# A place of its own for each weight slab: shifted split weights in a decoder step of one core

## The chip, the core and the metric

The kernel runs on one core of a Trainium2 chip. The core has a matrix engine (TensorE), three engines that work on vectors (VectorE, ScalarE, GpSimd), SyncE, which here issues the transfers, and 16 DMA engines. Data are worked on in an on-chip memory of 128 partitions; TensorE writes its sums to a second one, PSUM. The metric is the time of one execution in microseconds on the device, as the median of several runs: 1639.8 us before the change (three runs, 1639.6 to 1639.88).

## What is computed

One step of a decoder layer for 288 token rows (a prompt of 256 and 8 samples of 4), all float32:

```
h = RMSNorm(x);  P = h @ w_in          # split into conv, stick-breaking attention, memory attention, gates
y_A, y_B, y_M                           # three branches, each ending in a projection to D_MODEL = 2048
x = x + (g_A*y_A + g_B*y_B + g_M*y_M) @ w_o
x = x + relu(RMSNorm(x) @ w_up)^2 @ w_down      # D_FF = 8192
```

Beside it, the keys and values of 256 memory tokens are projected, and new cache rows are returned. Nearly all the work is the product of 288 columns of activations with weights that are read once.

## The kernel before, in words

**Slabs.** All weights lie in one array `wall` of 504 slabs, each 128 partitions by 1024 float32 (512 KB). A slab holds eight blocks of 128x128. Slabs 0 to 15 belong to the memory keys and values, 16 to 215 to w_in and the branch projections, 216 to 247 to w_o. From 248 on four rounds follow, each with an up stage (32 slabs of w_up) and a down stage (32 slabs of w_down): up stages at 248, 312, 376 and 440, down stages at 280, 344, 408 and 472.

**The split.** Products of full float32 precision are made of the reduced type fp32r. A weight w is written as h + l: `cast_weights` (line 303, ScalarE) casts the raw slab `wr` into a tile `wh`, and `sub_part` (line 314, VectorE) writes the rest, wr - wh, into `wl`. Activations are split in the same way into `.h` and `.l`. A block's product is three matmuls: wh with a.h, wh with a.l, wl with a.h. So a slab is 8 x 3 = 24 matmuls. They stand on line 486, in `chunk`, first the 16 with wh, then the 8 with wl; each loads 128 columns of weights and streams the 288 columns of an activation. The memory stage (line 539) does it the other way round: 128 columns of an activation are the weights, and 512 columns of wh or wl stream.

**The buffers.** There are four raw slabs (`wr`), four `wh` and four `wl`, used in turn. Activations lie in pool `a` (tiles of 320 words), where class `Acts` takes words 12 to 300 (`AHEAD = 12`) for the 288-column ones. After the branches the tiles of the pools `k4` and `s` are made into 16 "homes", pairs of places for an h and an l half (`make_homes`): the merged branches use them as the input of w_o, and each up stage writes its output into them (`up_tile`), which the down stage reads. The pools' sizes, a spare tile `gap` of 32 words among them, and the 12 words put the moving operand of every line-486 matmul 48 bytes in front of its weights, counted modulo 256 bytes; for the memory stage the distance is 0.

**The order.** The whole program is written in the order that a planner (`Order`) works out when the kernel is built: each step is a generator that asks for an engine with a cost, flags to wait for and buffers. The matmuls of `main` stand in their fixed order; the other engines' steps are placed by these costs. Weights are loaded by SyncE in slab order as raw buffers come free, and a `wh`/`wl` buffer is given back when its slab's last matmul is written.

Names in the profile: `pm` and `pa` are PSUM banks, `a` activations, `k` and `s` the homes, `t` temporaries.

Of the kernel before, what the change touches and what calls it, by code (L numbers as in the profile page):

```python
# [7 lines left out]
F32 = mybir.dt.float32  # L8
F32R = mybir.dt.float32r
# [5 lines left out]
P = 128  # L15
D_MODEL = 2048
KT = D_MODEL // P
# [4 lines left out]
T = NP + NS  # L22
# [13 lines left out]
SLAB = 8 * P  # L36
N_SLABS = 504
# [116 lines left out]
def dve(n, *flags, **take):  # L154
    return Ask("DVE", 0.18 + n / 920.0, flags, **take)


def act(n, *flags, **take):
    return Ask("ACT", 0.22 + n / 1200.0, flags, **take)
# [12 lines left out]


APART = 320
AHEAD = 12
VISIT, VISIT_K = 4, 8
MM = 0.131
MM_MEM = 0.226
# [3 lines left out]
def tile_decoder_step(ctx: ExitStack, tc: tile.TileContext, xT, memT, wall, cvec, kmat, ptab,  # L182
                      kpool, vpool, mkc, mvc, hist,
                      yT, oK, oV, oCp, oCs, oMK, oMV):
    nc = tc.nc
    PS = bass.MemoryType.PSUM
    bufs = {"wr": 4, "w": 4, "a": 75, "t": 11, "k4": 9, "s": 8, "pm": 4, "pa": 3, "pl": 1}

    def open_pool(name, n, space=None):
        if space is None:  # L190
            return ctx.enter_context(tc.tile_pool(name=name, bufs=n))
        return ctx.enter_context(tc.tile_pool(name=name, bufs=n, space=space))

    cpool = open_pool("const", 1)
    pools = {}
    for p, n in bufs.items():
        if p == "t":
            open_pool("gap", 1).tile([P, 32], F32, name="gap")
        if p != "w":
            pools[p] = open_pool(p, n, PS if p in ("pm", "pa", "pl") else None)  # L200
    pools["wh"] = open_pool("wh", bufs["w"])
# [6 lines left out]
    def tl(p, shape, dt=F32):  # L208
        cnt[0] += 1
        return pools[p].tile(shape, dt, tag=p, name=f"{p}_{cnt[0]}")  # L210
# [16 lines left out]


    nc.scalar.preload_act_table_set(LN_EXP)
    warm = pools["wh"].tile([P, SLAB], F32R, tag="wh", name="wh_0")  # L230
    order.pools["w"].pop()
    nc.gpsimd.memset(warm[:, :512].bitcast(F32), 1.0)
    eps = cpool.tile([P, 1], F32, name="eps")
    nc.gpsimd.memset(eps, EPS)
    ones = cpool.tile([P, P], F32, name="ones")
    nc.gpsimd.memset(ones, 1.0)
    ones_r = cpool.tile([P, P], F32R, name="ones_r")
    nc.vector.tensor_copy(ones_r, ones)
    ones_s = cpool.tile([P, T], F32, name="ones_s")
    nc.gpsimd.memset(ones_s, 1.0)  # L240
    cv = cpool.tile([P, NCV], F32, name="cv")
    nc.scalar.dma_start(cv[:, :C_BGATE], cvec[:, :C_BGATE])
    km = cpool.tile([P, NKM], F32, name="km")
# [4 lines left out]
    snew = km[:, K_SNEW:K_SNEW + NS]  # L248
    tri_r = cpool.tile([P, P], F32R, name="tri_r")
    rx = cpool.tile([P, T], F32, name="rx")  # L250
    r2 = cpool.tile([P, T], F32, name="r2")
    rm = cpool.tile([P, MT], F32, name="rm")
    nm = [cpool.tile([P, MT * MH], F32, name=f"nm{i}") for i in range(4)]
    sm_mx, sm_sum, sm_rc = (cpool.tile([P, 2], F32, name=f"sm{i}") for i in range(3))
# [25 lines left out]
    def load_slab(s, part):  # L280
# [4 lines left out]
        nc.sync.dma_start(sl.raw[:, part * n:(part + 1) * n], wall[s, :, part * n:(part + 1) * n])  # L285
        sl.landed[part].at = order.landed(n * P * 4 / 1e3)

    def due(s):
        return at_slab[1] + 2.9 * (s - at_slab[0])

# [2 lines left out]
    def cast_weights():  # L293
        todo = [(0, 0), (1, 0), (0, 1), (1, 1)] + [(s, i) for s in range(2, N_SLABS) for i in range(slabs[s].parts)]
        for s, i in todo:
            sl = slabs[s]
            n = SLAB // sl.parts
            cast_at[0] = s
            yield act(n, sl.landed[i], **({} if i else {"w": 1}))
            if i == 0:  # L300
                sl.h = tl("wh", [P, SLAB], F32R)
            c = slice(i * n, (i + 1) * n)
            nc.scalar.copy(sl.h[:, c], sl.raw[:, c])  # L303
            sl.split[i].cast = order.now.ready
            add(sub_part(s, i), lambda s=s: 0 if due(s) - order.free["DVE"] < 5.0 else 4.5)

    def sub_part(s, i):
        sl = slabs[s]
        n = SLAB // sl.parts
        yield dve(n, late=Order.HOP + 0.1)  # L310
        if i == 0:
            sl.l = tl("wl", [P, SLAB], F32R)
        c = slice(i * n, (i + 1) * n)
        nc.vector.tensor_sub(sl.l[:, c], sl.raw[:, c], sl.h[:, c].bitcast(F32))  # L314
        done(sl.split[i])
        if i == sl.parts - 1:
            give("wr")
# [5 lines left out]
    class Acts:  # L323


        def __init__(self, n=T):
            c = slice(AHEAD, AHEAD + n) if n == T else slice(0, n)
            self.h, self.l = tl("a", [P, APART], F32R)[:, c], tl("a", [P, APART], F32R)[:, c]
            self.flag = Flag()

# [176 lines left out]
    def main_tile(acts, evac, rank=1.0, n_slabs=2):  # L507
        yield pe(0.0, pm=1)
        ps = bank("pm")[:, :T]
        for i in range(n_slabs):  # L510
            slab_no[0] += 1
            yield from products(ps, FULL, acts[8 * i:8 * i + 8], i == 0, i == n_slabs - 1)
            give("w")
        add(evac(ps), rank)
# [720 lines left out]
    homes, homes_in = [], Flag()  # L1235
# [4 lines left out]

    def make_homes():
        yield sp(*conv_done, *osb_in, k4=bufs["k4"], s=bufs["s"])
        parts = []
        for _ in range(bufs["k4"]):
            x = tl("k4", [P, 1024], F32R)
            parts += [x[:, AHEAD + i * APART:AHEAD + i * APART + T] for i in range(3)]
        for _ in range(bufs["s"]):
            parts.append(tl("s", [P, 512], F32R)[:, AHEAD:AHEAD + T])
        for j in range(KT):
            homes.append(Home(parts[2 * j], parts[2 * j + 1]))  # L1250
        done(homes_in)


# [12 lines left out]
    merged = [None] * KT  # L1266

    def branch(br, j):
        def evac(ps):
            sig = gates[br, j]  # L1270
            if br == 2:
                yield dve(T, sig.flag, a=1)
                macc[j] = tl("a", [P, T])
                nc.vector.tensor_mul(macc[j], ps, sig.out)
                give("pm")
                give("t")
                return
            yield dve(T, sig.flag)
            nc.vector.tensor_mul(sig.out, ps, sig.out)
            give("pm")  # L1280
            yield dve(T)
            nc.vector.tensor_add(macc[j], macc[j], sig.out)
            give("t")
            if br == 0:
                yield act(T, homes_in)
                a = merged[j] = homes[j]
                nc.scalar.copy(a.h, macc[j])
                yield dve(T)
                nc.vector.tensor_sub(a.l, macc[j], a.h.bitcast(F32))
                give("a")  # L1290
                done(merged_in[j])
        return evac
# [41 lines left out]
        return load, evac  # L1334


    def up_tile(u, f):
        def evac(ps):
            yield dve(T, r2_done, t=1)
            r = tl("t", [P, T])  # L1340
            nc.vector.scalar_tensor_tensor(r, ps, 0.0, r2, op0=ALU.max, op1=ALU.mult)  # L1341
            give("pm")
            yield pool(T)
            nc.gpsimd.tensor_mul(r, r, r)  # L1344
            yield act(T)
            a = homes[f]
            nc.scalar.copy(a.h, r)  # L1347
            yield dve(T)
            nc.vector.tensor_sub(a.l, r, a.h.bitcast(F32))  # L1349
            give("t")  # L1350
            u[f].h, u[f].l = a.h, a.l
            done(u[f].flag)
        return evac
# [57 lines left out]
    def main():  # L1411
        yield from warm_up()
        yield from mem_products()
        yield from conv_products([evac_lin(0, "pa"), evac_gat(0, "pa"), evac_lin(1, "pm"), evac_gat(1, "pm")])
        for j in range(2, CT):
            yield from main_tile(hx, evac_lin(j, "pm"))
            yield from main_tile(hx, evac_gat(j, "pm"))
        add(samples(), 3.0)
        for h in range(MH):
            yield from main_tile(hx, mem_head(h), 2 + 0.05 * h)  # L1420
        for h in range(SH):
            yield from main_tile(hx, sb_key(h), 2.2 + 0.05 * h)
            yield from main_tile(hx, sb_query(h), 2.2 + 0.05 * h)
            yield from main_tile(hx, sb_head(h), 2.2 + 0.05 * h)
        yield from branch_products(2, [Late(omem, h, om_in[h]) for h in range(MH)])
        give("a", 8)
        yield from branch_products(1, [Late(osb, h, osb_in[h]) for h in range(SH)])
        give("a", 16)
        yield from branch_products(0, [Late(cact, j, cact_flags[j]) for j in range(CT)])
        give("a", 40)  # L1430
        mg = [Late(merged, j, merged_in[j]) for j in range(KT)]
        for j in range(KT):
            load, evac = out_tile(j)
            add(load(), 2)
            yield from main_tile(mg, evac)
        add(sum_norm(sq_sum, D_MODEL, r2, r2_done, sums_2), 0.4)
        hh = [Late(h2, j, h2_in[j]) for j in range(KT)]
        for c in range(D_FF // D_MODEL):
            u = [Later() for _ in range(KT)]
            for f in range(KT):  # L1440
                yield from main_tile(hh, up_tile(u, f))
            for j in range(KT):
                yield from main_tile(u, down_tile(j, c == D_FF // D_MODEL - 1))

# [174 lines left out]
```

## Time and profile before

| | |
|---|---|
| median of three runs | 1639.8 us |
| the profiled execution | 1639.4 us, its span 1637.6 us |
| TensorE matmuls | 12786, busy 1633.0 us (100%) |
| weight loads of TensorE | 12786, busy 1615.7 us (99%) |
| VectorE | 992.2 us (61%) |
| ScalarE | 739.3 us (45%) |
| GpSimd | 138.9 us (8%) |
| DMA | 305.39 MB, mean 186 GB/s |
| granted TensorE clock | 1.000 |

The span is the time from the first to the last instruction of the profiled execution; its own time has a little more around it. A matmul's record lasts from the start of its reading to the end of its writing, and the next one starts well before that; so the pace of matmuls is read from their starts, not from the durations. In rows of the chain and of the order in time, the first number is the start of a piece in us from the span's start, the second its length, and the number behind the x how many instructions it merges.

### The profile page before, as it was taken

How to read it: one execution, taken by the hardware profiler on the slowest of the kernel's cores; microseconds unless marked ns; L12 is line 12 of the kernel's file. 1: busy time of each engine (PE TensorE's matmuls, PEld its weight loads, DVE VectorE, ACT ScalarE, POOL GpSimd, SP SyncE). 2: the span in 40 equal slices, each digit the busy share in tenths (PEclk: the TensorE clock that was granted, in tenths of full speed). 3: DMA queues.
4: the chain of work that ended last, by engine and by line, in shares of the span. 5: the costliest groups of instructions: out<-in, count | busy, mean ns of one | idle time of the engine just before them, and what ended most of it. 6: DMA issues, size and time to landing. Idle time of an engine off the chain costs nothing.

```text
span 1637.6 us, 30963 instructions
## 1 busy us (share of the span) xinstructions
PE 1633.0 (100%) x12786; PEld 1615.7 (99%) x12786; DVE 992.2 (61%) x1471; ACT 739.3 (45%) x1070; POOL 138.9 (8%) x105
## 2 busy tenths in 40 slices
PE   9999999999999999999999999999999999999999
PEld 7999999999999999999999999999999999999999
DVE  8888888877777655565555544455445554455443
ACT  8746666644343534444443433333333333333332
POOL 0020000000000000001222200122001210022100
PEclk9999999999999999999999999999999999999999
DMA  9686465776755555556655555555555555555563
GB/s 339 217 184 248 148 203 195 251 257 243 256 162 167 152 184 174 169 162 202 193 175 167 170 169 173 170 168 170 167 169 168 169 173 170 169 168 168 179 192 100
DMA packets 107103, 305.39 MB, mean 186 GB/s; under 512 B 19922, under 2 KB 29522, under 8 KB 106962
## 3 DMA queue, kind: packets, MB, share of 16 engines
q1 hardware_dynamic: 106818, 303.39, 58.4%
q8 instruction: 100, 1.64, 0.4%
q14 instruction: 41, 0.34, 0.1%
q10 hardware_dynamic: 144, 0.02, 0.0%
HBM read 297.05 MB, written 6.32 MB: 185 GB/s over the span
## 4 chain that ended last, share of the span: by engine, by line
PE 100%; POOL 0%; DVE 0%; issue 0%; POOLq 0%
PE pm L486 93%; PE pm L539 3%; PE pa L486 1%; PE pl L1015 1%; PE pl L1188 0%; PE pa L852 0%; PE pa L853 0%; PE pa L851 0%; PE pl L1031 0%; PE pa L1407 0%; PE pa L825 0%; PE pa L1142 0%; PE pa L906 0%; PE pa L1139 0%; PE pa L1141 0%; PE pa L1106 0%
## 5 line engine op out<-in xcount | busy, mean ns | idle before, releaser
L303 ACT CAST wh<-wr 128x1024 fp32r<-128x1024 f32 (+1 forms) x520 | 530.5, 1023 | 652.1 <-PE pm L486 596.2
L486 PE MATMUL pm<-a,wh 128*128 128x288 f32 x5184 | 742.3, 293 | 0.0
L314 DVE TENSOR_TENSOR wl<-wr,wh 128x1024 fp32r<-128x1024 f32 (+1 forms) x520 | 616.6, 1189 | 197.2 <-ACT wh L303 192.4
L486 PEld LDWEIGHTS pm<-a,wh 128*128 128x128 f32 x5184 | 699.7, 188 | 1.3 <-issue 1.2
L486 PE MATMUL pm<-a,wl 128*128 128x288 f32 x2592 | 398.6, 293 | 0.0
L486 PEld LDWEIGHTS pm<-a,wl 128*128 128x128 f32 x2592 | 359.8, 188 | 0.0
L486 PE MATMUL pm<-k,wh 128*128 128x288 f32 x2160 | 306.8, 292 | 0.0
L486 PEld LDWEIGHTS pm<-k,wh 128*128 128x128 f32 x2160 | 290.2, 188 | 0.0
L486 PE MATMUL pm<-k,wl 128*128 128x288 f32 x1120 | 171.6, 292 | 0.0
L486 PEld LDWEIGHTS pm<-k,wl 128*128 128x128 f32 x1120 | 155.0, 188 | 0.0
L1344 POOL TENSOR_TENSOR t<-t 128x288 f32<-128x288 f32 x64 | 96.3, 1505 | 599.9 <-DVE t L1341 599.9
L1358 DVE TENSOR_TENSOR a<-a,pm 128x288 f32<-128x288 f32 x64 | 29.1, 454 | 122.5 <-PE pm L486 122.5
L1341 DVE SCALAR_TENSOR_TENSOR t<-pm,r 128x288 f32<-128x288 f32 x64 | 29.2, 458 | 90.3 <-PE pm L486 90.3
L1347 ACT CAST k<-t 128x288 fp32r<-128x288 f32 x56 | 24.2, 433 | 115.7 <-POOL t L1344 115.7
L1260 DVE TENSOR_TENSOR t<-pm,rx 128x288 f32<-128x288 f32 x48 | 22.0, 458 | 73.2 <-PE pm L486 73.2
L486 PE MATMUL pm<-s,wh 128*128 128x288 f32 x400 | 65.0, 293 | 0.0
L717 DVE SCALAR_TENSOR_TENSOR a<-a,cv,a 128x256 f32<-128x256 f32 x120 | 57.7, 481 | 1.4
L1330 POOL TENSOR_TENSOR t<-t,t 128x288 f32<-128x288 f32 x15 | 22.0, 1469 | 420.9 <-ACT t L1327 420.9
L486 PEld LDWEIGHTS pm<-s,wh 128*128 128x128 f32 x400 | 56.6, 188 | 0.0
L1349 DVE TENSOR_TENSOR k<-t,k 128x288 fp32r<-128x288 f32 x52 | 23.8, 458 | 51.1 <-ACT k L1347 51.1
L539 PE MATMUL pm<-wh,a 128*128 128x512 f32 x128 | 35.1, 396 | 0.0
L486 PE MATMUL pm<-s,wl 128*128 128x288 f32 x160 | 33.8, 293 | 0.0
(214 smaller groups left out, 785.5 us busy)
## 6 DMA issues: line engine op xcount, KB each, us to landing
wr<-in_wall SPq DMA_DIRECT2D x488, 512.0 KB, 3.6
wr<-in_wall SPq DMA_DIRECT2D x32, 256.0 KB, 4.8
k<-in_kpool SPq DMA_DIRECT2D x32, 256.0 KB, 6.0
k<-in_vpool SPq DMA_DIRECT2D x32, 256.0 KB, 5.9
k<-in_mkc SPq DMA_DIRECT2D x8, 512.0 KB, 8.8
k<-in_mvc SPq DMA_DIRECT2D x8, 512.0 KB, 6.4
t<-in_xT SPq DMA_DIRECT2D x16, 144.0 KB, 3.6
out_yT<-a SPq DMA_DIRECT2D x16, 144.0 KB, 1.8
```

The source lines that it names most:

```text
L303: nc.scalar.copy(sl.h[:, c], sl.raw[:, c])
L314: nc.vector.tensor_sub(sl.l[:, c], sl.raw[:, c], sl.h[:, c].bitcast(F32))
L486: nc.tensor.matmul(ps, w, a, start=(first and i == 0), stop=(last and i == len(todo) - 1))
L539: nc.tensor.matmul(ps[m], y[:, m * P:(m + 1) * P], z[:, w], start=(k == 0 and j < 2), stop=(k == KT - 1 and j in (4, 5)))
L717: nc.vector.scalar_tensor_tensor(c[:, :NP], up[:, k:k + NP], w, c[:, :NP], op0=ALU.mult, op1=ALU.add)
L1260: nc.vector.tensor_mul(g, ps, rx)
L1330: nc.gpsimd.tensor_add(sq_sum[0], sq_sum[0], res[0])
L1341: nc.vector.scalar_tensor_tensor(r, ps, 0.0, r2, op0=ALU.max, op1=ALU.mult)
L1344: nc.gpsimd.tensor_mul(r, r, r)
L1347: nc.scalar.copy(a.h, r)
L1349: nc.vector.tensor_sub(a.l, r, a.h.bitcast(F32))
L1358: nc.vector.tensor_add(x1[j], x1[j], ps)
```

## The change

Three things change together, all of them places of data in the partition.

- `wh` and `wl` buffers are 64 words (256 bytes) longer, and a table `SHIFT` gives the number of words by which each of the last 288 slabs (216 on) is moved forward in its buffers, the same for wh and wl.
- The activations' places: `AHEAD` is 4, the tile `gap` is gone, and the 16 homes exist in five sets of places (`PLACES`), one for w_o and one for each of the four rounds, with a start of its own for the h and the l half.
- To make room, the tile `ones` is dropped (its copy is read from `ones_s`), and `r2` uses the tile of `rx`.

As a result, counted modulo 256 bytes from the weights to the moving data: in slabs 16 to 215 the distance is 144 bytes instead of 48. In the first up stage it takes turns by slab between 144 and 96, in the second between 144 and 48, in the third between 96 and 48. In w_o, the four down stages and the last up stage it is given by lot. In w_o and the down stages each of 16 shifts, 16 bytes apart, occurs twice; in the last up stage the eight shifts 0, 5, 7, 11, 30, 32, 39 and 55 words occur four times each. The memory stage stays at distance 0.

No instruction changes its place in the order of TensorE, ScalarE, VectorE or SyncE; GpSimd has one fill fewer.

```diff
-AHEAD = 12
+AHEAD = 4
+PLACES = ((6, 6), (4, 12), (12, 4), (4, 0), (2, 2))
+SHIFT = (
+    10, 62, 34, 30, 54, 22, 30, 18, 38, 38, 18, 58, 26, 50, 62, 42, 58, 42, 34, 6, 2, 22, 54, 14,
+    26, 14, 46, 6, 46, 50, 2, 10, 0, 12, 0, 12, 0, 12, 0, 12, 0, 12, 0, 12, 0, 12, 0, 12,
...
+)
+PAD = 64
...
-        if p == "t":
-            open_pool("gap", 1).tile([P, 32], F32, name="gap")
...
-    warm = pools["wh"].tile([P, SLAB], F32R, tag="wh", name="wh_0")
+    warm = pools["wh"].tile([P, SLAB + PAD], F32R, tag="wh", name="wh_0")
...
-    ones = cpool.tile([P, P], F32, name="ones")
-    nc.gpsimd.memset(ones, 1.0)
-    ones_r = cpool.tile([P, P], F32R, name="ones_r")
-    nc.vector.tensor_copy(ones_r, ones)
     ones_s = cpool.tile([P, T], F32, name="ones_s")
     nc.gpsimd.memset(ones_s, 1.0)
+    ones_r = cpool.tile([P, P], F32R, name="ones_r")
+    nc.vector.tensor_copy(ones_r, ones_s[:, :P])
...
-    r2 = cpool.tile([P, T], F32, name="r2")
+    r2 = rx
...
+    def shifted(p, s):
+        n = SHIFT[s - N_SLABS + len(SHIFT)] if s >= N_SLABS - len(SHIFT) else 0
+        return tl(p, [P, SLAB + PAD], F32R)[:, n:n + SLAB]
...
-                sl.h = tl("wh", [P, SLAB], F32R)
+                sl.h = shifted("wh", s)
...
-            sl.l = tl("wl", [P, SLAB], F32R)
+            sl.l = shifted("wl", s)
...
-            c = slice(AHEAD, AHEAD + n) if n == T else slice(0, n)
+            c = slice(AHEAD, AHEAD + n) if n == T else slice(32, 32 + n)
...
-        for _ in range(bufs["k4"]):
-            x = tl("k4", [P, 1024], F32R)
-            parts += [x[:, AHEAD + i * APART:AHEAD + i * APART + T] for i in range(3)]
-        for _ in range(bufs["s"]):
-            parts.append(tl("s", [P, 512], F32R)[:, AHEAD:AHEAD + T])
-        for j in range(KT):
-            homes.append(Home(parts[2 * j], parts[2 * j + 1]))
+        big = [tl("k4", [P, 1024], F32R) for _ in range(bufs["k4"])]
+        small = [tl("s", [P, 512], F32R) for _ in range(bufs["s"])]
+        for place in PLACES:
+            parts = [[x[:, i * APART + n:i * APART + n + T] for x in big for i in range(3)] + [x[:, n:n + T] for x in small]
+                     for n in place]
+            homes.append([Home(parts[0][2 * j], parts[1][2 * j + 1]) for j in range(KT)])
...
-                a = merged[j] = homes[j]
+                a = merged[j] = homes[0][j]
...
-            a = homes[f]
+            a = homes[1 + c][f]
```

More of the change, by code (lines that the diff above doesn't have):

```diff
@@ L1242, in make_homes @@
         yield sp(*conv_done, *osb_in, k4=bufs["k4"], s=bufs["s"])
-        parts = []
-        for _ in range(bufs["k4"]):
-            x = tl("k4", [P, 1024], F32R)
-            parts += [x[:, AHEAD + i * APART:AHEAD + i * APART + T] for i in range(3)]
-        for _ in range(bufs["s"]):
-            parts.append(tl("s", [P, 512], F32R)[:, AHEAD:AHEAD + T])
-        for j in range(KT):
-            homes.append(Home(parts[2 * j], parts[2 * j + 1]))
+        big = [tl("k4", [P, 1024], F32R) for _ in range(bufs["k4"])]
[4 more added lines that the diff above has]
+            homes.append([Home(parts[0][2 * j], parts[1][2 * j + 1]) for j in range(KT)])
         done(homes_in)
@@ L1334, in out_tile, with up_tile @@
         return load, evac
-    def up_tile(u, f):
+    def up_tile(u, f, c):
         def evac(ps):
@@ L1440, in main @@
             for f in range(KT):
-                yield from main_tile(hh, up_tile(u, f))
+                yield from main_tile(hh, up_tile(u, f, c))
             for j in range(KT):
```

10 rows, old and new, of the table SHIFT are left out of this document.

## The prediction

> **What bounds the kernel now.** I read the page first (busy shares), then the chain that ended last in order of time, then the order of single instructions on TensorE, and last the groups of ScalarE and VectorE.
>
> ```profile
> span 1637.6 us, 30963 instructions
> ...
> PE 1633.0 (100%) x12786; PEld 1615.7 (99%) x12786; DVE 992.2 (61%) x1471; ACT 739.3 (45%) x1070; POOL 138.9 (8%) x105
> ...
> PEclk9999999999999999999999999999999999999999
> ...
> PE 100%; POOL 0%; DVE 0%; issue 0%; POOLq 0%
> PE pm L486 93%; PE pm L539 3%; PE pa L486 1%; PE pl L1015 1%; PE pl L1188 0%; PE pa L852 0%; PE pa L853 0%; PE pa L851 0%; PE pl L1031 0%; PE pa L1407 0%; PE pa L825 0%; PE pa L1142 0%; PE pa L906 0%; PE pa L1139 0%; PE pa L1141 0%; PE pa L1106 0%
> ```
>
> TensorE is busy for the whole span at full clock, and the chain is TensorE alone: 94% of it the matmuls of line 486, each 128 weight columns against 288 moving columns. The only thing that can move the time by much is the pace of those matmuls, that is the time from one start to the next. The next rows (start, length, instructions of a piece of the chain) give it.
>
> ```profile
> 364.66 29.41 PE pm L486 x222
> ...
> 439.71 84.27 PE pm L486 x636
> 524.24 22.26 PE pm L486 x168
> 546.77 297.18 PE pm L486 x2286
> 844.22 790.16 PE pm L486 x6078
> ```
>
> 84.27/636 = 132.5 ns, 29.41/222 = 132.5 and 22.26/168 = 132.5; but 297.18/2286 = 130.0 and 790.16/6078 = 130.0. The same instruction, with operands at the same distance in the partition, runs at one of two paces, and nothing waits inside either piece. So something inside a matmul costs time that a wait does not show. Closer up (start, length, count):
>
> ```profile
> 62.17 0.70 PE L486 MATMUL pa<-a,wh 128*128 128x288 f32 x4
> 62.71 0.42 PE L486 MATMUL pa<-a,wl 128*128 128x288 f32 x2
> 62.97 0.70 PE L486 MATMUL pa<-a,wh 128*128 128x288 f32 x4
> 63.51 0.42 PE L486 MATMUL pa<-a,wl 128*128 128x288 f32 x2
> 63.77 0.69 PE L486 MATMUL pm<-a,wh 128*128 128x288 f32 x4
> 64.29 0.44 PE L486 MATMUL pm<-a,wl 128*128 128x288 f32 x2
> 64.57 0.69 PE L486 MATMUL pm<-a,wh 128*128 128x288 f32 x4
> ...
> 600.17 1.20 PE L486 MATMUL pm<-a,wl 128*128 128x288 f32 x8
> 601.21 2.24 PE L486 MATMUL pm<-a,wh 128*128 128x288 f32 x16
> 603.29 1.20 PE L486 MATMUL pm<-a,wl 128*128 128x288 f32 x8
> ```
>
> At 62 us the spacing moves about: 0.54/4 = 135, 0.26/2 = 130, then 130 (0.52/4) and 140 (0.28/2). At 600 us it is even: 1.04/8 and 2.08/16, both 130. A last row for scale is the memory stage, 512 moving columns, weights and moving data at equal places modulo 256 bytes.
>
> ```profile
> 39.48 1.07 PE L539 MATMUL pm<-wh,a 128*128 128x512 f32 x4
> 40.39 0.61 PE L539 MATMUL pm<-wl,a 128*128 128x512 f32 x2
> 40.84 1.07 PE L539 MATMUL pm<-wh,a 128*128 128x512 f32 x4
> ```
>
> 1.36 us for six, 226.7 ns each, or 0.443 ns a column; 288 columns at that rate would be 127.5 ns. So a 288-column matmul has 2.5 to 5 ns over what the longest one pays per column.
>
> **The change, part by part.** No instruction is added to TensorE, ScalarE or SyncE and their order is the same; GpSimd loses one fill (the tile of ones) and VectorE's order is the same with one tile renamed (r2 is rx). What changes is where in the partition the operands lie. Counted from the buffers' starts, all modulo 256 bytes: before, the moving data of every line-486 matmul lies 48 bytes in front of its weights. After, it lies
>
> - 144 bytes in front in slabs 16 to 215 (4800 matmuls: 200 slabs of 24);
> - 144 and 96, then 144 and 48, then 96 and 48, taking turns by slab, in the first three up stages (96 slabs, 2304 matmuls; one in two of the second and third stage keeps 48, so 1536 matmuls are moved);
> - at a drawn distance in w_o, the four down stages and the last up stage (192 slabs, 4608 matmuls). The draws are even: each of 16 places twice in 32 slabs, or in the last up stage each of eight places four times, six of them off the 16-byte grid (5, 7, 11, 30, 39 and 55 words).
>
> The trace has no other distance for this shape, so each price is bounded by its nearest rows. The low end is 127.5 ns (the 512-column rate), the high end 135 ns (the group of four at 62.17). For a matmul moved to a place nobody has measured I take the middle of the two sustained paces, (130.0 + 132.5)/2 = 131.25: those rows have the same shape and are nearest. Against 130.0, where all slabs from 216 on run now, that is +1.25 ns.
>
> The early stretch, constant 144. Before 546.77 us lie 11712 - 2286 - 6078 = 3348 of the 11712 line-486 matmuls, and the rows above show 636 + 222 + 168 = 1026 of them at 132.5. The stretch already mixes both paces, so I take 0. Ends: if 144 gives 130.0 throughout, at most 3348 x 2.5 = 8.4 us less; if it gives 132.5 throughout, at most (4800 - 1026) x 2.5 = 9.4 us more.
>
> The up stages: 1536 x 1.25 = +1.9 us; ends -1536 x 2.5 = -3.8 and +1536 x 2.5 = +3.8 (132.5).
>
> The drawn slabs: 4608 x 1.25 = +5.8 us; ends -4608 x 2.5 = -11.5 and +4608 x 5.0 = +23.0 (135).
>
> The memory stage (192 matmuls) keeps distance 0, since its tiles now start 32 words in: 0.
>
> The split itself: the cast and the subtraction write the same shapes at shifted places. What covers them is their slack.
>
> ```profile
> L303 ACT CAST wh<-wr 128x1024 fp32r<-128x1024 f32 (+1 forms) x520 | 530.5, 1023 | 652.1 <-PE pm L486 596.2
> ...
> L314 DVE TENSOR_TENSOR wl<-wr,wh 128x1024 fp32r<-128x1024 f32 (+1 forms) x520 | 616.6, 1189 | 197.2 <-ACT wh L303 192.4
> ```
>
> A slab lasts 24 x 130 = 3.12 us on TensorE. ScalarE spends 1.02 us of it on the cast and then waits for TensorE to free the buffer (596.2 us in all); VectorE spends 1.19 us and waits for the cast. Were an odd start to double both, the two in a row would take 4.4 us, but on two engines and over four buffers, so still under 3.12 each: 0. If that cover were gone, each 0.1 us of slab pace would cost 288 x 0.1 = 29 us, and TensorE would show waits for wl; I see no reason for it. The longer buffers change only addresses. The shared r2/rx tile is written after the last gate has read it, a whole w_o stage earlier: 0. The copy into ones_r now follows the longer fill of ones_s, at the very start.
>
> ```profile
> L238 DVE CAST ones_r<-ones x1: 324/324/324, 1.5 to 1.5; 128x128 fp32r<-128x128 f32 x1
> ```
>
> It ran at 1.5 us, and its first reader is a row sum after the first loads, so a delay of a µs is hidden: 0.
>
> Sum: 0 + 1.9 + 5.8 = +7.7 us. The profiled execution took 1639.4 us (span 1637.6 and 1.8 around it), 0.4 under the median 1639.8 of three. 1639.4 + 7.7 = 1647.1 us.
>
> The Trainium skill, "TensorE: Matmul & The Clock Gate", Part 2 (Step-by-step), says that TensorE reads its moving operand and its weights through two independent read ports, and "SBUF — State Buffer" (SBUF: two separate sides) that TensorE never waits on anyone there. By that rule no distance between the two operands matters and the sum is 0, so 1639.4. The 132.5 and 130.0 ns above are at one distance, so they neither prove nor refute it; they do exceed the 122.5 ns that the first page's formula for the back-to-back issue gap gives for 288 columns (an estimate), so something it leaves out is at work.
>
> **The rivals.**
>
> Faster: the constant 144 keeps the early stretch out of the uneven 132.5 pace, and drawn slabs average what 48 gives. For it: the slow pace is seen only in one kind of state, which a change of place may break, and the second piece of the chain shows that 130.0 can hold for 6078 matmuls. Against: the slow pace came and went at one distance, so distance alone doesn't choose it. Price: -8.4 us at most, so 1631. It decides once the moved slabs cost less on average than 8.4/6144 = 1.4 ns each.
>
> ```profile
> L486 PE MATMUL pm<-a,wh 128*128 128x288 f32 x5184 | 742.3, 293 | 0.0
> ...
> L486 PEld LDWEIGHTS pm<-a,wh 128*128 128x128 f32 x5184 | 699.7, 188 | 1.3 <-issue 1.2
> ...
> L486 PE MATMUL pm<-k,wh 128*128 128x288 f32 x2160 | 306.8, 292 | 0.0
> ...
> L486 PE MATMUL pm<-s,wh 128*128 128x288 f32 x400 | 65.0, 293 | 0.0
> ```
>
> No effect of place: the overhead is a fixed cost of each matmul (switching weights, or filling). For it: at 600 us the pace is the same with wh and wl, whose addresses are 16 KB apart, and in the groups just shown a, k and s operands all take 292 to 293 ns from start to end. Against: those all keep the distance of 48, so none of them tests it. Time: 1639.4.
>
> Much slower: at some distances the two reads meet over the whole weight load, and those slabs run at the 135 to 140 seen singly at 62 us; weights off the 16-byte grid need a line more each. Price: the upper ends, 23.0 + 3.8 + 9.4 = 36, so up to 1676; with the early stretch as it is, 1666. For it: a weight load's record lasts 188 ns and one begins every 130, so a load is always under way beside a matmul and a slower one has no gap to fall into. Against: averages over evenly drawn places take good ones with the bad.
>
> **How the numbers follow.** Forecast, somewhat slower (1643 to 1660): 0.46. Faster by the early stretch or by better places: 0.29. No effect of place: 0.14. Much slower (over 1660): 0.11. About 0.2%, 3.3 us, is what this measurement tells from no change. Of the no-effect case 0.01 may fall below that band and 0.01 above it, and 0.01 of the forecast inside it. So faster 0.29 + 0.01 = 0.30, same 0.14 - 0.02 + 0.01 = 0.13, slower 0.46 - 0.01 + 0.11 + 0.01 = 0.57. The range of 8 in 10 takes the forecast, the no-effect case and most of the faster one: 1629 to 1661. The forecast's own range is 1643 to 1660.
>
> **What would show it right or wrong.** The chain should again be TensorE alone, with line 486 at 94%. In its pieces, the early stretch (to about 735 us) should show paces between 130.0 and 132.5; from 735 us on, slabs of different drawn places should have different paces, averaging about 131.25, and the stages that take turns should lie between. If every slab after 735 us still starts a matmul each 130.0 ns, place doesn't matter. If some drawn slabs come under 129 and few over 132, the rival that ends faster is right. If TensorE shows waits for wl or wh, the split has become the bound, which I costed at nothing. The prediction is wrong on its first step if the two paces are set by something else than the reads of the two operands.

## The result, and the profile after

The changed kernel takes 1648.1 us (median of four runs, 1648.0 to 1648.3) against 1639.8 before: ratio 1.0051, 95% interval 1.0033 to 1.0068. It is 8.3 us slower, within the range forecast (1629 to 1661) and 1.0 us from the predicted 1647.1.

The page of the changed kernel, whose line 502 is line 486 of before (and 319 and 330 are 303 and 314):

```profile
span 1646.2 us, 30962 instructions
...
PE 1641.2 (100%) x12786; PEld 1623.6 (99%) x12786; DVE 991.8 (60%) x1471; ACT 738.3 (45%) x1070; POOL 138.8 (8%) x104
...
PEclk9999999999999999999999999999999999999999
...
PE 99%; DMA 0%; SPq 0%; ACT 0%; DVE 0%; issue 0%
PE pm L502 93%; PE pm L555 3%; PE pa L502 1%; PE pl L1031 1%; PE pl L1204 0%; PE pa L868 0%; PE pa L869 0%; PE pa L867 0%; DMA wr<-in_wall 0%; PE pl L1047 0%; PE pa L841 0%; PE pa L1158 0%; PE pa L922 0%; PE pa L1155 0%; PE pa L1157 0%; PE pa L1122 0%
...
L319 ACT CAST wh<-wr 128x1024 fp32r<-128x1024 f32 (+1 forms) x520 | 529.5, 1021 | 661.5 <-PE pm L502 608.0
...
L330 DVE TENSOR_TENSOR wl<-wr,wh 128x1024 fp32r<-128x1024 f32 (+1 forms) x520 | 616.5, 1189 | 200.5 <-ACT wh L319 197.1
```

TensorE is still nearly the whole chain (99%; the chain now starts with 4.28 us of a weight transfer instead of seven matmuls of line 1407) at full clock, and a slab's split costs what it did (1.02 and 1.19 us, with nearly the same waits for TensorE: 608.0 us against 596.2). So the 8.6 us of span lie inside the matmuls. The chain in order of time (start, length, count):

```profile
362.76 28.86 PE pm L502 x222
...
437.25 82.69 PE pm L502 x636
520.21 21.84 PE pm L502 x168
542.31 300.30 PE pm L502 x2286
842.88 800.11 PE pm L502 x6078
```

The pieces that ran at 132.5 ns before now run at 130.0 (82.69/636, 28.86/222, 21.84/168). The pieces that ran at 130.0 before are slower: 800.11/6078 = 131.6. The two effects have opposite signs. The first matmul that reads a home is the start of w_o (the last two times of these lines are first and last start, the first line before, the second after):

```profile
L486 PE MATMUL pm<-k,wh x2160: 292/292/293, 735.4 to 1632.4; 128*128 128x288 f32 x197
L502 PE MATMUL pm<-k,wh x2160: 289/295/310, 730.9 to 1640.9; 128*128 128x288 f32 x197
```

w_o began at 735.4 us before and begins at 730.9 now, so the early stretch, memory stage included, gained 4.5 us; from there to the span's end it was 902.2 us and is 915.3, so the rest lost 13.1.

By stage ("grid" is the 16-byte grid of addresses), as the mean time from one start to the next (steps over 160 ns, real stalls, left out), and the excess over 130.0 ns times the matmuls of the stage:

| stage | distance, bytes | before, ns | after, ns | excess after, us |
|---|---|---|---|---|
| slabs 16 to 215 | 144 | 131.2 | 130.1 | 0.7 (before 5.4) |
| w_o | lot, all 8 bytes off the grid | 130.0 | 134.0 | 3.1 |
| up 1, 2, 3 | 144/96, 144/48, 96/48 | 130.0 | 130.6, 131.3, 130.1 | 0.5, 1.0, 0.1 |
| down 1, 2, 3 | lot, h and l apart | 130.0 | 132.2, 132.1, 132.6 | 1.7, 1.6, 2.0 |
| up 4 | lot, weights off the grid in six of eight shifts | 130.0 | 130.4 | 0.3 |
| down 4 | lot, all 8 bytes off the grid | 130.0 | 133.7 | 2.9 |

The turns can be seen slab by slab. In the second up stage (start, length, count, in the order of time) a slab with wh at distance 144 begins at 1048.49 and one at 48 at 1051.61:

```profile
1048.49 2.24 PE L502 MATMUL pm<-a,wh 128*128 128x288 f32 x16
1050.57 1.20 PE L502 MATMUL pm<-a,wl 128*128 128x288 f32 x8
1051.61 2.28 PE L502 MATMUL pm<-a,wh 128*128 128x288 f32 x16
1053.73 1.22 PE L502 MATMUL pm<-a,wl 128*128 128x288 f32 x8
1054.79 1.46 PE L502 MATMUL pm<-a,wh 128*128 128x288 f32 x10
```

From 1048.49 to 1051.61 are 24 matmuls at 130.0 ns, from 1051.61 to 1054.79 are 24 at 132.5. Same instruction, neighbouring slabs, only the place differs. Place alone is not all of it: in the third up stage, where slabs at 48 take turns with slabs at 96, the slabs at 48 run at 130.2.

### The profile page after: what moved, and what is told of

It is laid out like the page before. It is cut to its first block, busy times and chain, and to the rows that moved or that the text cites. A ratio compares the mean times of both kernels' runs of the same rounds, so it can differ in the third digit from the quotient of the medians.

```text
span 1646.2 us, 30962 instructions
## 1 busy us (share of the span) xinstructions
PE 1641.2 (100%) x12786; PEld 1623.6 (99%) x12786; DVE 991.8 (60%) x1471; ACT 738.3 (45%) x1070; POOL 138.8 (8%) x104
## 4 chain that ended last, share of the span: by engine, by line
PE 99%; DMA 0%; SPq 0%; ACT 0%; DVE 0%; issue 0%
PE pm L502 93%; PE pm L555 3%; PE pa L502 1%; PE pl L1031 1%; PE pl L1204 0%; PE pa L868 0%; PE pa L869 0%; PE pa L867 0%; DMA wr<-in_wall 0%; PE pl L1047 0%; PE pa L841 0%; PE pa L1158 0%; PE pa L922 0%; PE pa L1155 0%; PE pa L1157 0%; PE pa L1122 0%
## 5 line engine op out<-in xcount | busy, mean ns | idle before, releaser
L319 ACT CAST wh<-wr 128x1024 fp32r<-128x1024 f32 (+1 forms) x520 | 529.5, 1021 | 661.5 <-PE pm L502 608.0
L502 PE MATMUL pm<-k,wh 128*128 128x288 f32 x2160 | 313.4, 295 | 0.0
L502 PEld LDWEIGHTS pm<-k,wh 128*128 128x128 f32 x2160 | 296.3, 189 | 0.0
L1355 DVE SCALAR_TENSOR_TENSOR t<-pm,rx 128x288 f32<-128x288 f32 x64 | 29.3, 458 | 92.3 <-PE pm L502 92.3
```

The costliest lines, as they stand in the source:

```text
L502: nc.tensor.matmul(ps, w, a, start=(first and i == 0), stop=(last and i == len(todo) - 1))
```

## The experiments

All keep the changed kernel's order of instructions unless the text says otherwise. Where only the table of shifts and the starts of the homes differ, a pace can be read from each stage; a table of shifts with one number a stage is written as repeats of that number.

**One distance for all.** Every slab at 144 bytes.

```diff
-PLACES = ((6, 6), (4, 12), (12, 4), (4, 0), (2, 2))
+PLACES = ((4, 4), (4, 4), (4, 4), (4, 4), (4, 4))
-SHIFT = (
...
-)
+SHIFT = ((32,) * 32 + (0,) * 32) * 4 + (32,) * 32
```

> All line-502 matmuls at one distance, 144 bytes (slabs of w_o and of the down stages shifted by 32 words, all others by 0, homes at 4 words). If 144 is a place at which the slow pace of 132.5 ns does not arise (what the changed kernel's early stretch shows), every stage runs at 130.0 ns and the time is that of before less the early stretch's excess, 1639.8 - 5 = 1634 to 1636 us. If a constant distance can fall into the slow pace at any place, as it did at 48 before 546 us, some stages show 132.5 and the time is 1639 us or more.

Measured 1635.7 us, ratio to before 0.9972 (0.9961 to 0.9983). All nine stages from w_o on run at 130.0 ns, the early stretch at 130.1. The last pieces of its chain:

```profile
437.93 82.69 PE pm L499 x636
520.89 21.84 PE pm L499 x168
542.99 297.20 PE pm L499 x2286
840.46 790.22 PE pm L499 x6078
```

790.22/6078 = 130.0, as before the change, so the gain over before, 4.3 us, is the early stretch's alone. The longer buffers, the shared tile and the dropped fill cost nothing that shows.

**The lot, with all homes on the grid.** Same distances, slab by slab; in w_o and the last down stage both operands moved back by 2 words, and h and l at one place in the other down stages.

```diff
-PLACES = ((6, 6), (4, 12), (12, 4), (4, 0), (2, 2))
+PLACES = ((4, 4), (4, 4), (4, 4), (4, 4), (0, 0))
-    10, 62, 34, 30, 54, 22, 30, 18, 38, 38, 18, 58, 26, 50, 62, 42, 58, 42, 34, 6, 2, 22, 54, 14,
...
+    8, 60, 32, 28, 52, 20, 28, 16, 36, 36, 16, 56, 24, 48, 60, 40, 56, 40, 32, 4, 0, 20, 52, 12, 24, 12, 44, 4, 44, 48, 0, 8,
...
```

> The changed kernel's drawn places stay as they are (same distances, same order), but the homes start on the 16-byte grid in every stage and at the same place for the h and the l half. Theory A (where the moving data start is what costs: 8 bytes off the 16-byte grid in w_o and the last down stage, h and l apart in the other three): w_o and all four down stages fall from 132.1 to 134.0 ns to about 130.4, as in the last up stage, and the time is about 1648.1 - 10 = 1638 us. Theory B (the drawn distances are what costs): w_o and the down stages stay above 132 ns and the time stays within 3 us of 1648.

Measured 1645.3 us, ratio 1.0032 (1.002 to 1.0044). w_o 132.0, down stages 132.1, 131.9, 132.0 and 132.4. So the drawn distances cost some 2.0 ns by themselves (theory B). Theory A foretold some 130.4 in all of them and fails as a whole, but it holds for a part: coming back onto the grid is worth 2.0 ns in w_o (134.0 to 132.0) and 1.4 ns in the last down stage, 2.6 us together. h and l apart, in the other three, cost at most 0.6 ns.

**No lot, the homes as changed.**

```diff
-SHIFT = (
...
-)
+SHIFT = (34,) * 32 + ((0,) * 32 + (32,) * 32) * 3 + (0,) * 32 + (30,) * 32
```

> No lot: every stage has one distance from slab to slab, but the homes keep the changed kernel's starts. w_o and the last down stage are 8 bytes off the 16-byte grid on both sides at distance 144; down stages 1 to 3 have h and l apart (144/176, 176/144, 144/128); the up stages stay at 144. Theory A: w_o and the last down stage 133 to 134 ns, down stages 1 to 3 about 132, time about 1645 us. Theory B: all stages 130.0 ns and 1635 us, as with one constant distance.

Measured 1646.4 us, ratio 1.0037 (1.0024 to 1.0051). w_o, 8 bytes off at distance 144, ran at 135.0, the last down stage at 133.4, down stages 1 to 3 at 132.0, 132.5 and 131.8, the up stages at 130.0 to 130.1. Three rows of w_o, 24 matmuls from the first to the third, 3.24/24 = 135.0 ns:

```profile
744.09 2.32 PE L499 MATMUL pm<-k,wh 128*128 128x288 f32 x16
746.25 1.24 PE L499 MATMUL pm<-k,wl 128*128 128x288 f32 x8
747.33 0.97 PE L499 MATMUL pm<-k,wh 128*128 128x288 f32 x6
```

Being 8 bytes off the grid costs without any lot. For h and l apart the reading is less simple: their l half lies at 176 or 128, and the next runs show that these distances have prices of their own.

**A map of settings, constant in each stage.** Three kernels, one run each; every fence shows the new values alone, which stand in the place of the old `PLACES` and the old table `SHIFT`. The first also tries operands off the grid by 4, 8 and 12 bytes.

```diff
+PLACES = ((4, 4), (5, 5), (7, 7), (5, 5), (2, 2))
+SHIFT = tuple(n for n in (34, 24, 32, 12, 32, 32, 33, 40, 28) for _ in range(32))
```

> One fixed setting a stage, to read a pace from each. w_o: weights 8 bytes off the grid, moving data on it; last down stage: moving data 8 bytes off, weights on it; down stages 1 and 2: moving data 4 and 12 bytes off, weights on it; down stage 3: both 4 bytes off. Up stages at constant distances 48, 96, 16 and 240. Theory A: about 130 ns in w_o (as weights off the grid cost nothing in the last up stage) and 133 or more in the four down stages. Theory B: 130.0 in all of these, as nothing is drawn. The up stages: 130.0 if the distance only matters when it changes from slab to slab; 132.5 at some if a distance by itself can bring the slow pace (48 did before 546 us; 16 was at 131.7 when drawn).

The second:

```diff
+PLACES = ((0, 0), (8, 8), (12, 12), (20, 20), (28, 28))
+SHIFT = tuple(n for n in (28, 36, 36, 28, 40, 20, 48, 16, 56) for _ in range(32))
```

> Which matters, the distance or the place itself? w_o and the four down stages all keep distance 144, on the 16-byte grid, but with the moving data and the weights together at 0, 8, 12, 20 and 28 words. If the distance alone counts (on the grid), all five run at 130.0 ns. If the place itself counts, some do not. The up stages add distances to the map, one each: 0, 32, 64 and 80. From the drawn slabs of the kernel with all homes on the grid, where 16 even places averaged 132.0 to 132.4, most of these should lie between 131 and 133.5.

The third:

```diff
+PLACES = ((4, 4), (4, 4), (4, 4), (4, 4), (4, 4))
+SHIFT = tuple(n for n in (40, 48, 36, 44, 28, 2, 24, 5, 20) for _ in range(32))
```

> One constant distance a stage, homes at 4 words: w_o 112, down stages 128, 160, 176 and 192, up stages 208, 224, 136 and 124 (the last two with weights off the 16-byte grid). If each distance has a price of its own, as 48 (130.2), 96 (131.1), 16 (131.7) and 240 (132.0) had when constant, the on-grid stages lie between 130 and 135 and the mean over all 16 distances is about 132.0, the pace of the slabs given by lot. If the lot itself costs (the change from slab to slab), the constant distances average 130.0 to 131 and the lot's 132.0 is not explained by them.

Measured, with both operands on the grid and one distance a stage (moving data at word 4 of a home or an up stage's input):

| distance | 0 | 16 | 32 | 48 | 64 | 80 | 96 | 112 |
|---|---|---|---|---|---|---|---|---|
| ns | 130.7 | 131.7 | 133.3 | 130.2 | 133.3 | 131.1 | 131.1 | 133.3 |

| distance | 128 | 144 | 160 | 176 | 192 | 208 | 224 | 240 |
|---|---|---|---|---|---|---|---|---|
| ns | 133.3 | 130.0 | 131.7 | 131.4 | 132.4 | 133.3 | 131.7 | 132.0 |

The mean of the sixteen is 131.9, and the lot on the grid ran at 131.9 to 132.4. So on average the lot costs nothing of its own: a stage of it takes the mean of the prices of its distances, of which 48 and 144 are the two cheapest. Slab by slab it does not hold: in the lot on the grid six of the eight slabs at 160 that read the homes at word 4 ran at 133.2 to 133.5, against 131.7 when that distance was constant in the same homes. Even 144 isn't immune: one slab there, in w_o behind a slab at 112, took 3.20/24 = 133.3 ns:

```profile
788.67 2.29 PE L499 MATMUL pm<-k,wh 128*128 128x288 f32 x16
790.81 1.23 PE L499 MATMUL pm<-k,wl 128*128 128x288 f32 x8
791.87 1.61 PE L499 MATMUL pm<-k,wh 128*128 128x288 f32 x11
```

Three rows at distance 64 (third up stage of the second kernel; 24 matmuls from the first to the third row):

```profile
1250.60 2.30 PE L499 MATMUL pm<-a,wh 128*128 128x288 f32 x16
1252.73 1.23 PE L499 MATMUL pm<-a,wl 128*128 128x288 f32 x8
1253.80 2.30 PE L499 MATMUL pm<-a,wh 128*128 128x288 f32 x16
```

Again 3.20/24 = 133.3 ns. But the distance isn't all: at 144, with both operands moved together, homes at words 12 and 28 gave 130.0, at 20 131.1, at 0 and 8 132.2. And off the grid isn't always dear: moving data 12 bytes off ran at 130.0 (distance 156), 4 bytes off at 134.7 and, with the weights 4 off too, 134.2, 8 bytes off at 133.3; weights off the grid alone gave 132.2 at distance 136 in two places and 130.0 at 124. The Trainium skill, "TensorE: Matmul & The Clock Gate", Part 2 (Step-by-step), gives TensorE two independent read ports for the two operands; these runs differ from what that would lead one to expect, 130.0 to 135.0 ns with nothing changed but places.

**The early stretch put back to 48.** The changed kernel, with the weights of slabs 16 to 215 moved forward by 24 words.

```diff
-        n = SHIFT[s - N_SLABS + len(SHIFT)] if s >= N_SLABS - len(SHIFT) else 0
+        n = SHIFT[s - N_SLABS + len(SHIFT)] if s >= N_SLABS - len(SHIFT) else 24 if s >= KT else 0
```

> The changed kernel with its first part undone: the weights of slabs 16 to 215 are moved forward by 24 words, so that the early stretch has distance 48 again, as before the change; the rest stays as it is. If the 132.5 ns pace belongs to distance 48, it comes back in the early stretch and the time is about 1648.1 + 5 = 1653 us. If the early stretch's gain came from something else (the places of the raw slabs, the pools' other addresses), the stretch stays at 130.0 and the time at 1648 us.

Measured 1650.3 us, 2.2 more than the changed kernel (ratio to before 1.0062, 1.0045 to 1.0079); w_o began at 733.0 us instead of 730.9. So distance 48 is dearer there, but by less than half of what I expected: the piece of 636 matmuls kept 130.0, and only the piece of 168 went back to 132.5 (22.26/168).

```profile
438.94 82.68 PE pm L499 x636
521.89 22.26 PE pm L499 x168
```

**Distance 48 at the places of before.** In the longer buffers, with the spare tile put ahead of pool `a`.

```diff
-AHEAD = 4
-PLACES = ((6, 6), (4, 12), (12, 4), (4, 0), (2, 2))
+AHEAD = 12
+PLACES = ((12, 12), (12, 12), (12, 12), (12, 12), (12, 12))
...
+SHIFT = ((0,) * 32 + (32,) * 32) * 4 + (0,) * 32
...
+        if p == "a":
+            open_pool("gap", 1).tile([P, 32], F32, name="gap")
...
-        n = SHIFT[s - N_SLABS + len(SHIFT)] if s >= N_SLABS - len(SHIFT) else 0
+        n = SHIFT[s - N_SLABS + len(SHIFT)] if s >= N_SLABS - len(SHIFT) else 32
...
-            c = slice(AHEAD, AHEAD + n) if n == T else slice(32, 32 + n)
+            c = slice(AHEAD, AHEAD + n) if n == T else slice(0, n)
```

> The run with the early distance put back to 48 lost 2.2 us, not 5, and its pieces of 636 and 168 matmuls did not all return to 132.5 ns; its operands had the distance of before but lay 96 bytes further on. This kernel has the longer buffers and gives distance 48 at the very places of before, modulo 256 bytes (144 for the moving data, 96 for the weights in slabs 16 to 215 and the up stages; 16 and 224 in w_o and the down stages). If the slow pace belongs to those places, the early pieces show 132.5 again and the time is about 1640 us. If it came from the shorter buffers (their steps of 4096 bytes) or from other addresses, the pieces show 130 and the time is about 1636 us.

Measured 1655.3 us, ratio 1.0094 (1.0078 to 1.0109): neither of the two. The early piece of 636 shows 132.5 again, and the last piece too:

```profile
438.80 84.27 PE pm L501 x636
...
844.99 805.37 PE pm L501 x6078
```

805.37/6078 = 132.5. The matmuls ran at 130.0 from some 530 us to 734 us, went over to 132.5 where w_o began, and never came back, also in up stages whose distance and places were those of before. That needed a new theory: at 48 a matmul has two paces, and which of them holds is carried on.

**One place for all, and then a nudge in each stage.** Two kernels, the first told against the one just shown, the second against the first. The homes at word 44 with shift 32 everywhere give distance 48 at one place. The second kernel moves one slab in the middle of each stage from the first up stage on to another distance.

```diff
-PLACES = ((12, 12), (12, 12), (12, 12), (12, 12), (12, 12))
+PLACES = ((44, 44), (44, 44), (44, 44), (44, 44), (44, 44))
...
-SHIFT = ((0,) * 32 + (32,) * 32) * 4 + (0,) * 32
+SHIFT = (32,) * 288
```

```diff
-SHIFT = (32,) * 288
+SHIFT = tuple(x for n in (32, 8, 20, 8, 20, 40, 20, 44, 20) for x in (32,) * 16 + (n,) + (32,) * 15)
```

> In the run with the places of before, the matmuls at distance 48 ran at 130.0 ns up to 734 us, went over to 132.5 as w_o began (where the homes lay 128 bytes on) and stayed there to the end, also in the up stages, whose places were those of before. This kernel has one place for all: moving data at 144, weights at 96 modulo 256, homes too, in the longer buffers. Theory C (at distance 48 a matmul has two paces, and which one holds is carried from matmul to matmul until something disturbs it): with nothing that changes between stages the pace it has at 600 us holds to the end, as in the kernel before, and the time is either about 1638 to 1640 us (130.0) or about 1655 (132.5), with no stage in between. Theory D (the longer buffers, or the place of the homes, bring 132.5): 132.5 ns from w_o on, 1655 us.

> The same, with one slab (24 matmuls) at another distance in the middle of each stage from the first up stage on: 144, 96, 144, 96, 16, 96, 0, 96, in the order of the program. Theory C: the pace of the slabs at 48 changes only at such a slab and then stays to the next one; as in the changed kernel slabs at 48 ran at 132.5 right behind slabs at 144 and at 130.2 behind slabs at 96, a slab at 144 should leave 132.5 behind it and one at 96 should leave 130.0. Theory D: the single slabs change nothing beyond their own 24 matmuls.

One place for all: 1637.8 us, ratio 0.9988 (0.9978 to 0.9997), all stages from w_o on at 130.0. With the nudges: 1651.8 us (one run). The two pieces, first without and then with nudges:

```profile
843.00 790.16 PE pm L501 x6078
```

```profile
842.52 804.25 PE pm L501 x6078
```

The 24 matmuls at 144 begin at 883.70, in the second kernel:

```profile
880.59 2.24 PE L501 MATMUL pm<-a,wh 128*128 128x288 f32 x16
882.66 1.20 PE L501 MATMUL pm<-a,wl 128*128 128x288 f32 x8
883.70 2.24 PE L501 MATMUL pm<-a,wh 128*128 128x288 f32 x16
885.78 1.20 PE L501 MATMUL pm<-a,wl 128*128 128x288 f32 x8
886.83 2.28 PE L501 MATMUL pm<-a,wh 128*128 128x288 f32 x16
888.95 1.22 PE L501 MATMUL pm<-a,wl 128*128 128x288 f32 x8
890.01 2.28 PE L501 MATMUL pm<-a,wh 128*128 128x288 f32 x16
```

Up to 886.83 the slabs take 3.11 to 3.13 us (130 ns a matmul); from there each takes 3.18 (132.5), and the slabs at 48 keep that to the end. One slab of 24 matmuls at another place made all later ones at 48 slower by 2.5 ns: theory C for this half, in a single run of the kernel, but with the step at exactly that slab. It speaks against theory D too, which has the longer buffers or the place of the homes bring 132.5: with both unchanged the matmuls ran at 130.0 up to this slab. The other half of theory C failed: the slabs at 96 (and at 16 and 0) ran at 131.2 to 131.6 themselves and did not bring 130.0 back.

Distance 96 has two paces as well, in the changed kernel already: 131.1 ns in the first up stage, where it takes turns with 144, and 130.1 in the third, where it takes turns with 48. One reading fits all of these: a slab at 144 leaves the slower pace behind it, and a slab at 96 passes on the one that it found. No run tests this on purpose, so it stays a reading.

**What is left in the 130.0.** All at 144; the low products of each stage with fewer columns, so part of the sums is left out.

```diff
+COLS = (288, 272, 256, 224, 192, 160, 128, 96, 64)
...
-        for i, (w, a) in enumerate(todo):
-            nc.tensor.matmul(ps, w, a, start=(first and i == 0), stop=(last and i == len(todo) - 1))
+        for i, (w, a, *x) in enumerate(todo):
+            x = x and x[0]
+            end = last and i == len(todo) - 1
+            n = T if end or not x else COLS[max(0, (slab_no[0] - 1 - 216) // 32)]
+            nc.tensor.matmul(ps[:, :n], w, a[:, :n], start=(first and i == 0), stop=end)
...
-            chunk(ps, [(w[:, c:c + P], a.l if x else a.h) for w, c, a, x in part],
+            chunk(ps, [(w[:, c:c + P], a.l if x else a.h, w is sl.l) for w, c, a, x in part],
```

> What is in the 130.0 ns that the best distance leaves? All at distance 144; from the first up stage on, the matmuls with wl (but the last of each sum) take only the first 272, 256, 224, 192, 160, 128, 96 and 64 columns, one number a stage in the order of the program, so part of the low products is left out. If the overhead is a fixed time of each matmul beside one column a cycle (10 ns beside 120), the spacing of the shortened ones falls by 1 ns for each 2.4 columns: 123.3 at 272, 116.7 at 256, 103.3 at 224. If it goes with the columns (0.451 ns each), 122.8, 115.6 and 101.1. Where the weight load sets the pace it stops falling; the memory stage's 128-column neighbours came at 108.5 ns, so below some 200 columns I expect about 108.

Measured 1608.7 us (one run). The first short matmul behind full ones was followed after 123, 117, 102, 88, 72, 58, 44 and 29 ns (272 down to 64 columns, medians). That is within 2 ns of the form that goes with the columns (0.451 ns each: 122.8 down to 28.9) and up to 8 ns from the form with a fixed 10 ns, which falls by 1 ns for each 2.4 columns, to 36.7 at 64. The short ones behind it fit neither: they came about 124 and 119 ns apart at 272 and 256 columns, and mostly 107 to 117 apart at 224 and fewer, however few. Five starts at 64 columns, from 1554.83 to 1555.39:

```profile
1554.83 0.72 PE L503 MATMUL pm<-k,wl 128*128 128x64 f32 x5
1555.39 0.49 PE L503 MATMUL pm<-s,wl 128*128 128x64 f32 x2
```

0.56/5 = 112 ns. The weight loads begin 108 to 112 ns apart there too, so my reading is that a load takes that long, that one can be ahead, and that a load fills most of the 130 ns beside a 288-column matmul. Another fixed cost of each pair of load and matmul would look the same, and no run tells the two apart. That the 130.0 goes with the columns is what the first short ones say; there is no run in which every matmul is shorter.

**The gain with four edits of places.** The kernel before, in buffers of the old length.

```diff
-AHEAD = 12
+AHEAD, HOME = 4, 36
...
-        if p == "t":
-            open_pool("gap", 1).tile([P, 32], F32, name="gap")
...
-            c = slice(AHEAD, AHEAD + n) if n == T else slice(0, n)
+            c = slice(AHEAD, AHEAD + n) if n == T else slice(32, 32 + n)
...
-            parts += [x[:, AHEAD + i * APART:AHEAD + i * APART + T] for i in range(3)]
+            parts += [x[:, HOME + i * APART:HOME + i * APART + T] for i in range(3)]
...
-            parts.append(tl("s", [P, 512], F32R)[:, AHEAD:AHEAD + T])
+            parts.append(tl("s", [P, 512], F32R)[:, HOME:HOME + T])
```

> The kernel before with four edits of places and nothing else: the spare tile gone, activations from word 4, homes from word 36, the memory tiles from word 32. Distance 144 everywhere in buffers of the old length, both operands 128 bytes further on than in the run with one constant distance of 144. If distance and places modulo 128 bytes decide, every stage runs at 130.0 ns and the time is that run's, 1635.7 us. If the longer buffers or the place modulo 256 matter, it is above 1637.

Measured 1635.6 us, ratio 0.9974 (0.9964 to 0.9984): 4.3 us faster than the kernel before and faster than the changed one, in buffers no longer than before. All stages from w_o on at 130.0, the early stretch at 130.2.

```profile
438.13 82.69 PE pm L484 x636
521.09 21.84 PE pm L484 x168
543.20 297.18 PE pm L484 x2286
840.64 790.15 PE pm L484 x6078
```

## Why the prediction came out

The total was right, 7.7 us forecast and 8.3 measured, but two of its terms were wrong, by about 4.5 us less and 5.7 us more, and nearly cancelled. That the total came within 1.0 us is luck; that the kernel got slower because drawn places cost more than 48 did is not.

- **What bounds the kernel.** Right: TensorE at full clock, and the pace of its matmuls alone.
- **The early stretch, 0.** Wrong: it gained 4.5 us, inside the bound of 8.4. This is the step that failed: I took the mixture of two paces as given for any distance. The run with 144 throughout shows that it need not be: 144 holds 130.0 there, 48 can fall into 132.5.
- **The up stages, +1.9.** About right: 0.5, 1.0 and 0.1, together 1.5 us before rounding. Of its parts, the slabs at 48 in the second stage, which the sum had left at 130.0, ran at 132.4, so here too the sum came out better than its parts.
- **The drawn slabs, +5.8.** The mechanism was right, the size half: 3.1, 1.7, 1.6, 2.0, 0.3 and 2.9, together 11.5 us before rounding, within the end of 23.0. The term mis-sized is 131.25 ns for an unmeasured place; the 4608 matmuls took 132.5 on average. Evenly drawn distances cost 131.9 on the grid, and both operands 8 bytes off cost 1.4 to 2.0 ns more in two of the six stages (2.6 us), which the sum did not have as a price.
- **The low end, 127.5 ns**, taken from the 512-column rate, was seen in no stage; 130.0 was the lowest mean of a stage in every run with 288 columns. Of the price at the other side, 135, one stage was that slow (w_o with one distance, 8 bytes off).
- **The split, 0, and the rest, 0.** Right: equal durations and waits, and the run with one distance was no slower anywhere.
- **The rivals.** The one that ends faster had its first half right (the early stretch) and its second wrong (drawn places don't average what 48 gives). No effect of place is refuted by the turns in one stage. Much slower: some places are dearer, but by no more than 5 ns as the mean of a stage, and whether two reads meet there isn't shown; weights off the grid were cheap in the last up stage (130.4), against what it supposed, though not at distance 136 (132.2).

What stays open is why a place has its price. The runs show that it depends on the distance, on the place and on what ran before, not which accesses meet.

## What to carry to other kernels

Where one engine is busy throughout and waits for nothing, compare the start-to-start pace of the same instruction between stages: here 2.5 ns in 130 made 4 us early, and 15 us where it held to the end. Try operand places one at a time, constant in each stage, and prefer one that mostly holds its pace beside other places (144 here, 130.0 to 130.1 in turns with 96 and 48) to one that has it only as long as nothing disturbs it (48). A lot gives about the mean of the prices, so it is never the best choice.

## What the runs showed that I had not expected

At distance 48 the pace is a state, that is, it depends on what ran before: the same instructions at the same places ran at 130.0 or 132.5 ns for over 6000 matmuls, and a single slab of 24 at another distance was enough to lengthen a piece of 6078 by 14 us (790.16 to 804.25). The kernel before owes its 130.0 after 546 us to that state. The dearest constant distances on the grid all came out at the same 133.3 ns (32, 64, 112, 128 and 208).
